# A hybrid encoder layer on one core: the feed-forward in two phases, and an opening without GpSimd

## The chip, the core and the metric

The kernel runs on one core of a Trainium2 chip. The core has a matrix engine (TensorE, PE in the profile, with its weight loads shown apart as PEld), three engines for elementwise work (VectorE = DVE, ScalarE = ACT, GpSimd = POOL) and a queue engine (SyncE = SP) that here issues every transfer between device memory (DRAM) and the on-chip memory (SBUF). Matmul results go to eight banks of an accumulation memory (PSUM), from which DVE and ACT copy them. The metric is device time in microseconds, the median of some runs; lower is better. The profile is one further execution.

## What is computed

One layer of an encoder for 1024 prompt tokens and 8 x 16 sample tokens, all treated as 1152 rows of width 1024 in single precision. An input layer norm, one wide projection, three mixers, a merge and a layer norm come first; then the convolutional feed-forward, which the change is about. From the reference:

```python
def causal_dwconv(u, buf, w):
    width = w.shape[0]
    t = u.shape[1]
    full = jnp.concatenate([buf.astype(u.dtype), u], axis=1)
    out = full[:, 0:t] * w[0]
    for j in range(1, width):
        out = out + full[:, j:j + t] * w[j]
    return out, full[:, t:]
...
    x = layer_norm(ALPHA * x + mix @ w_out, ln1_g, ln1_b)

    up, new_ffn_conv = causal_dwconv(x @ w_up, buf_ffn, f_conv_w)
    gate, val = jnp.split(up + f_conv_b, 2, axis=-1)
    x = layer_norm(ALPHA * x + (jax.nn.silu(gate) * val) @ w_down, ln2_g, ln2_b)
```

`w_up` is 1024 x 5632 (2816 gate and 2816 value columns), `w_down` is 2816 x 1024.

## The kernel before

**Tiles.** Rows (tokens) come in three blocks of 384 (`n`, 0 to 2), features in pieces of 128. Every matrix product is made of three matmuls on numbers split in two: high part times high part, low times high, high times low. A split is a cast on one engine (the high part) and a subtraction (the low part). A projection block (`block`, for one 128-column piece of weights and one row block) is 8 x 3 = 24 matmuls of 128x128 by 128x384. A weight piece is loaded raw (`wraw`, two buffers), cast by ACT (L205) and subtracted by DVE (L206) into `whl` (two buffers).

**Order.** Code is written in program order with side generators (`beside`) that advance one step at each `tick`, that is after every second contraction step of the matmuls. A planner then orders the instructions of each engine by its own simulation of time; within an engine, and within the SP queue, the order is fixed at build time and each instruction waits for its inputs and for the buffers that it overwrites.

**Opening** (L126 to L445). Nine row tiles of x are loaded (`load_x`, tag `xt`, six buffers). For each third, `ln_in` takes statistics on DVE (`ln_group`, L319 to L308), normalises (DVE for the first two tiles of the first third, else ACT), and `to_features` (L336) transposes on PE (L147), scales on ACT (L343), casts on DVE (L344) and subtracts on DVE and POOL in turn (L345). The first two projection units (`q_unit`) run in the order unit 0, unit 1 for each third, two PSUM banks (`g`) between them. The statistics of the second third are tied to follow the small operations of the first (`issue_after(ready[-1])`).

**Feed-forward** (L1658 to the end). For each of 22 pairs (128 gate columns, 128 value columns), the evictions `ev_half` copy the block to `xp` (ACT, L1743), convolve (ACT L1759, DVE L1762 twice), apply SiLU (L1765), multiply (DVE, L1769) and split the product into `g` tiles (L1773, L1774), which stay in SBUF (24 buffers). After two pairs of up-projection, `down` multiplies the two pairs before them with their rows of `w_down` (`late`, two split weight tiles) and adds the result to the residual sum `yac` (L1807). For one row tile and one half of the columns that is 2 x 3 matmuls of 128x128 by 128x512. The last `down` takes four pairs, adds with a row sum (L1817), and `last_ln` follows for each row tile: ACT and DVE for the first eight, and for the last one a chain on DVE and ACT with high priority (L1855 to L1864), with its stores at the end. `residual` loads the rows of the first norm back into `yac` and scales them (L1689, L1690) right after the first four up-projection blocks.

Of the kernel before, what the change touches and what calls it, by code (L numbers as in the profile page):

```python
# [71 lines left out]
def tile_encoder_step(ctx: ExitStack, tc: tile.TileContext, cst, x_prompt, x_sample, cache_k, cache_v, st_hgrn,  # L72
# [8 lines left out]
    wp = ctx.enter_context(tc.tile_pool(name="wp", bufs=2))  # L81
    s0 = ctx.enter_context(tc.tile_pool(name="s0", bufs=16 * NBLK))
# [85 lines left out]


# [3 lines left out]
    def vec_rows(items):  # L173
        with tc.tile_pool(name=nm("vst"), bufs=1) as vst:
            st = vst.tile([96, P], F32, name=nm("vstage"))
            r0 = sum(nv)
            r = 0
            for n, ap in items:
                k = ap.shape[0]
                load(st[r:r + k, :], ap)  # L180
                vo[n] = r0 + r
                r += k
            nv.append(r)
            ps = psum("ms")
            tr(ps[:, :r], st[:r, :])
            V.tensor_copy(vec[:, r0:r0 + r], ps[:, :r])
# [12 lines left out]
    def prep(pieces, kt=KD, cols=P):  # L199
# [4 lines left out]
        hl = wp.tile([P, 2, KD, P], F32R, tag="whl", name=nm("whl"), bufs=2)  # L204
# [27 lines left out]
    def block(hl, xh, xl, n, evict, kt=KD):  # L232
# [3 lines left out]
        for k in range(kt):  # L236
# [98 lines left out]

    def to_features(pool, xns, n, gname, bname, hi, lo):  # L336

        for k in range(KD):
# [6 lines left out]
            (G if k % 2 else V).tensor_sub(lo[k][n], x32, hi[k][n].bitcast(F32))  # L345
# [11 lines left out]
    def ln_in(n):  # L357
# [3 lines left out]
        for i, (t, (mu, rs)) in enumerate(zip(xts, st)):  # L361
            nb, r = (ln_st[:, 3 * n + i, j:j + 1] for j in range(2))
            if n == 0 and i < 2:
                V.tensor_scalar(t, t, mu, rs, ALU.subtract, ALU.mult)
            V.scalar_tensor_tensor(nb, mu, -1.0, rs, ALU.mult, ALU.mult)
            last = V.tensor_copy(r, rs)
            if n or i == 2:
                S.activation(t, t, AF.Identity, bias=nb, scale=r)  # L368
        ready.append(last.ins)
        yield from to_features(lambda: lp.tile([P, NW], F32, tag="x32", name=nm("x32"), bufs=4), xts, n, "ling", "linb",  # L370
                               hh, hl_)

# [1286 lines left out]
    late = ExitStack()  # L1659
# [17 lines left out]
    late_w = lambda: fp.tile([P, 2, D], F32R, tag="late", name=nm("late"), bufs=2)  # L1677
    yac = []

    def residual():  # L1680
        gb = late_w().bitcast(F32)
        for i, src in enumerate((ln1_g[0], ln1_b[0])):
            load(gb[:, i], src.partition_broadcast(P))
        yield 2
        S.mul(gb, gb, ALPHA)
        for j in range(NT):
            yac.append(yp.tile([P, D], F32, name=f"yac{j}"))
            load(yac[j], d_xn1[j * P:(j + 1) * P, :])
            V.tensor_mul(yac[j], yac[j], gb[:, 0])  # L1689
            V.tensor_add(yac[j], yac[j], gb[:, 1])  # L1690
            yield 3


# [18 lines left out]
    def ffn_pair(i):  # L1712
        pr = Head()
        pr.gate, pr.l36 = {}, None
        pr.gh, pr.gl = [None] * NBLK, [None] * NBLK

        def tail():
            yield 5
            ps1 = psum("ms")
            tr(ps1[:36, :P], pr.l36)  # L1720
            r36 = fp.tile([36, P], F32, tag="r36", name=nm("r36"), bufs=1)
            V.tensor_copy(r36, ps1[:36, :P])
            for hf in range(2):
                c0 = hf * DFF + i * P
# [3 lines left out]
        def ev_half(half):  # L1728
            st = {}
            ct = half * NFF + i  # L1730

            def ev(n, ps):
                last = n == NBLK - 1
                w = FW - 2 if last else NW
                xp = fpiece("xp", 3, FW)
                if n == 0:
                    V.memset(xp[:, 0:2], 0.0)
                    if half == 0 and i % 4 == 0:
                        beside(ffn_states(i))
                else:  # L1740
                    V.tensor_copy(xp[:, 0:2], st["carry"])
                if not last:
                    S.copy(xp[:, 2:2 + NW], ps)  # L1743
                    cr = fpiece("carry", 3, 2)
                    V.tensor_copy(cr, xp[:, NW:NW + 2])
                    st["carry"] = cr
                else:
                    if half == 0:
                        pr.l36 = fpiece("l36", 2, 36)
                    xv = bt(xp[:, 2 + FPW:FW], 2 + TB)  # L1750
                    V.tensor_copy(xv[:, :, 0:2], bt(old[i][half], 2))
                    S.copy(xp[:, 2:2 + FPW], ps[:, :FPW])
                    S.copy(xv[:, :, 2:], bt(ps[:, FPW:]))
                    V.tensor_copy(pr.l36[:, 2 * half:2 * half + 2], xp[:, FPW:FPW + 2])
                    V.tensor_copy(bt(pr.l36[:, 4 + 16 * half:20 + 16 * half], 2), xv[:, :, TB:])
                    if half:
                        beside(tail())
                acc = fpiece("ga", 4, FW) if half == 0 else fpiece("va", 2, FW)
                S.activation(acc[:, :w], xp[:, 2:2 + w], AF.Identity, scale=fvec[:, 2, ct:ct + 1],  # L1759
                             bias=fvec[:, 3, ct:ct + 1])  # L1760
                for j in range(2):
                    V.scalar_tensor_tensor(acc[:, :w], xp[:, j:j + w], fvec[:, j, ct:ct + 1], acc[:, :w],  # L1762
                                           ALU.mult, ALU.add)
                if half == 0:
                    S.activation(acc[:, :w], acc[:, :w], AF.Silu)  # L1765
                    pr.gate[n] = acc
                    return
                ga = pr.gate[n]
                V.tensor_mul(ga[:, :w], ga[:, :w], acc[:, :w])  # L1769
                gh, gl = fpiece("g", 24, NW, F32R), fpiece("g", 24, NW, F32R)  # L1770
                pr.gh[n], pr.gl[n] = gh, gl
                if not last:
                    S.copy(gh, ga[:, :w])  # L1773
                    V.tensor_sub(gl, ga[:, :w], gh.bitcast(F32))  # L1774
                else:
                    S.copy(gh[:, :FPW], ga[:, :FPW])
                    V.tensor_sub(gl[:, :FPW], ga[:, :FPW], gh[:, :FPW].bitcast(F32))
                    gv = bt(ga[:, 2 + FPW:FW], 2 + TB)[:, :, :TB]
                    S.copy(bt(gh[:, FPW:]), gv)
# [155 lines left out]
```

## Time and profile before

| | us |
|---|---|
| median of 3 runs (2264.65 to 2267.57) | 2264.73 |
| profiled execution | 2265.47 |
| its span, first to last instruction | 2263.7 |
| TensorE busy in the span | 2204.9 |
| VectorE busy | 1494.3 |
| ScalarE busy | 957.5 |
| GpSimd busy | 27.4 |

The mean granted clock of TensorE is 0.991 of full speed. The profile names an instruction by the line that issued it, its engine, operation and tiles (output<-inputs); all matmuls share L107 and all transposes L147, since a helper issues them. "Idle before <-X" is how long the engine stood before the instruction, and what ended that. The stretches that matter in the text are the opening (0 to about 60 us), the entry into the feed-forward (about 1430 to 1460), the feed-forward (to 2250) and the tail (from 2250).

### The profile page before, as it was taken

Reading aid. Unit: us, or ns where it says so; the run is one execution under the profiler, and the core shown is the slowest. Engines: PE = TensorE matmul, PEld = TensorE weight load, DVE = VectorE, ACT = ScalarE, POOL = GpSimd, SP = SyncE. Lnnn points to the kernel's source line nnn. Section 1 sums busy time; section 2 is a strip of 40 time slices with the busy share of each in tenths; the row PEclk is TensorE's granted clock in tenths of the full one; section 3 lists DMA queues with packets and bytes.
Section 4 is the critical chain, followed back from the end, with each engine's and each line's share of the span. In section 5 each row is a group of like instructions: output and inputs, shape, how many; then the busy total and the mean of one; then the engine's idle time right before and its main releaser. Section 6 shows DMA issues by size and latency. Waiting matters only on the chain.

```text
span 2263.7 us, 34662 instructions
## 1 busy us (share of the span) xinstructions
PE 2204.9 (97%) x12959; PEld 2060.0 (91%) x12959; DVE 1494.3 (66%) x4292; ACT 957.5 (42%) x2195; POOL 27.4 (1%) x28
## 2 busy tenths in 40 slices
PE   6999989999999999999999899999999999999997
PEld 6998889999999999999989888899999999999996
DVE  8267556666675657767878786776566656655667
ACT  4356434334444436365432333453334323433347
POOL 2000000000000000000000001000000000000000
PEclk9999999999999999999999999999999999999998
DMA  4121231222232221312354542321101110111022
GB/s 135 47 77 53 89 94 47 80 75 62 64 84 61 68 68 41 102 36 68 103 175 131 173 151 75 135 67 49 38 29 58 48 41 28 57 48 48 20 66 85
DMA packets 223929, 168.36 MB, mean 74 GB/s; under 512 B 34650, under 2 KB 213504, under 8 KB 223744
## 3 DMA queue, kind: packets, MB, share of 16 engines
q1 hardware_dynamic: 223760, 166.14, 24.5%
q8 instruction: 102, 1.67, 0.3%
q14 instruction: 67, 0.55, 0.1%
HBM read 126.91 MB, written 40.11 MB: 74 GB/s over the span
## 4 chain that ended last, share of the span: by engine, by line
PE 91%; DVE 4%; ACT 3%; issue 1%; DMA 1%; POOLq 0%; SPq 0%; POOL 0%; DVEq 0%; ACTq 0%
PE psg L107 78%; PE psp L107 5%; PE psch L107 4%; PE psp L147 1%; PE psms L107 1%; PE psch L147 1%; PE psms L147 1%; DMA xp<-d_o 0%; ACT L1199 0%; ACT L1195 0%; DVE o L1455 0%; DVE whl L206 0%; DMA vstage<-in_ln_in_b_dram 0%; ACT k L1195 0%; ACT xt L368 0%
## 5 line engine op out<-in xcount | busy, mean ns | idle before, releaser
L107 PE MATMUL psg<-hh,whl 128*128 128x384 f32 x2976 | 809.2, 345 | 1.4 <-DVE r27c L823 0.7
L107 PEld LDWEIGHTS psg<-hh,whl 128*128 128x128 f32 x2976 | 536.2, 189 | 15.3 <-issue 8.6
L107 PE MATMUL psg<-x1h,whl 128*128 128x384 f32 x2112 | 543.7, 336 | 0.9 <-ACT whl L205 0.9
L107 PE MATMUL psg<-hl,whl 128*128 128x384 f32 x1488 | 509.0, 342 | 1.2 <-POOL hl L345 1.2
L107 PEld LDWEIGHTS psg<-x1h,whl 128*128 128x128 f32 x2112 | 383.4, 188 | 3.3 <-ACT whl L205 1.4
L107 PE MATMUL psg<-x1l,whl 128*128 128x384 f32 x1056 | 354.8, 336 | 2.3 <-POOL x1l L345 1.3
L107 PEld LDWEIGHTS psg<-hl,whl 128*128 128x128 f32 x1488 | 280.6, 189 | 6.1 <-issue 2.6
L107 PE MATMUL psg<-late,g 128*128 128x512 f32 x1080 | 251.1, 391 | 0.0
L107 PEld LDWEIGHTS psg<-late,g 128*128 128x128 f32 x1080 | 201.9, 188 | 42.8
L107 PEld LDWEIGHTS psg<-x1l,whl 128*128 128x128 f32 x1056 | 199.3, 189 | 3.3 <-POOL x1l L345 1.6
L206 DVE TENSOR_TENSOR whl<-wraw,whl 128x1024 fp32r<-128x1024 f32 (+1 forms) x122 | 140.6, 1153 | 62.4 <-ACT whl L205 60.8
L1807 DVE TENSOR_TENSOR yac<-yac,psg 128x512 f32<-128x512 f32 x164 | 112.8, 688 | 89.7 <-PE psg L107 86.1
L107 PE MATMUL psg<-o,whl 128*128 128x384 f32 x720 | 141.7, 348 | 5.1 <-ACT o L1454 2.8
L205 ACT CAST whl<-wraw 128x1024 fp32r<-128x1024 f32 (+1 forms) x122 | 121.4, 996 | 59.7 <-PE psg L107 40.1
L107 PEld LDWEIGHTS psg<-o,whl 128*128 128x128 f32 x720 | 126.7, 193 | 7.7 <-ACT o L1454 3.4
L1762 DVE SCALAR_TENSOR_TENSOR va<-xp,fvec,va 128x384 f32<-128x384 f32 x132 | 82.0, 621 | 19.8 <-ACT va L1759 18.1
L107 PE MATMUL psg<-wres,mixh 128*128 128x512 f32 x288 | 92.3, 394 | 0.0
L1762 DVE SCALAR_TENSOR_TENSOR ga<-xp,fvec,ga 128x384 f32<-128x384 f32 x132 | 81.5, 619 | 11.6 <-ACT ga L1759 9.9
L1791 ACT CAST late<-wraw 128x1024 fp32r<-128x1024 f32 x20 | 20.1, 1047 | 162.5 <-PE psg L107 162.5
L1743 ACT COPY xp<-psg 128x384 f32<-128x384 f32 x88 | 42.2, 480 | 108.4 <-PE psg L107 108.0
L1421 ACT ACTIVATE ga<-psg 128x384 f32<-128x384 f32 x72 | 35.4, 491 | 99.3 <-PE psg L107 76.6
L854 DVE SCALAR_TENSOR_TENSOR acc<-xp,vec,acc 128x384 f32<-128x384 f32 (+1 forms) x108 | 64.8, 619 | 3.2 <-ACT acc L852 2.7
(468 smaller groups left out, 3104.3 us busy)
## 6 DMA issues: line engine op xcount, KB each, us to landing
wraw<-in_w_in_dram SPq DMA_DIRECT2D x58, 512.0 KB
wraw<-in_w_up_dram SPq DMA_DIRECT2D x44, 512.0 KB
d_g<-ga SPq DMA_DIRECT2D x72, 192.0 KB
wraw<-in_w_down_dram SPq DMA_DIRECT2D x22, 512.0 KB
acc<-d_g SPq DMA_DIRECT2D x48, 192.0 KB
d_o<-sq SPq DMA_DIRECT2D x24, 192.0 KB
xp<-d_o SPq DMA_DIRECT2D x24, 192.0 KB
x<-d_g SPq DMA_DIRECT2D x24, 192.0 KB
```

The source lines that it names most:

```text
L107: PE.matmul(out, lhsT, rhs, start=start, stop=stop)
L147: PE.transpose(out, in_, ident[:n, :n])
L205: S.copy(hl[:, 0, :kt, :cols], raw[:, :kt, :cols])
L206: V.tensor_sub(hl[:, 1, :kt, :cols], raw[:, :kt, :cols], hl[:, 0, :kt, :cols].bitcast(F32))
L854: V.scalar_tensor_tensor(acc[:, :w], xp[:, j:j + w], vcol("gcw", 12 * j + ci), acc[:, :w], ALU.mult, ALU.add)
L1421: S.activation(g, ps, AF.Tanh, scale=0.5)
L1743: S.copy(xp[:, 2:2 + NW], ps)
L1762: V.scalar_tensor_tensor(acc[:, :w], xp[:, j:j + w], fvec[:, j, ct:ct + 1], acc[:, :w], ALU.mult, ALU.add)
L1791: S.copy(hl[:, 0], raw)
L1807: V.tensor_add(yac[j][:, cs], yac[j][:, cs], ps)
```

## The change

The feed-forward becomes two phases. In the first, all 44 up-projection units run, and each pair's gated product is stored to DRAM (`d_gu`, 22 tensors of 128 x 1152). Then the pools of the first phase (`wp`, `s0`, `fp`) are closed and a pool `dp` and eight PSUM banks (`g`) are opened. The second phase makes two passes over the 22 row pieces of `w_down`, eleven each; a pass takes the three row blocks in turn, loads and splits the gated pieces (`gr`, `gd`), and keeps six sums in PSUM, for three row tiles and two column halves, over all eleven pieces. Weights are loaded and split at the first row block of a pass (`wdr`, `wd`, 12 buffers). The last row block of the second pass goes one sum at a time. `residual` moves to the second phase; the last norm's affine vectors are two whole tiles.

In the opening the low part is always subtracted on DVE; the statistics of the next third are tied to follow the last split of this one; `xt` has four buffers; the first three units run third by third, two of them interleaved by contraction step (`two_blocks`), with a third weight tile; the first tile of each third is normalised on ACT, the others on DVE; 20 matmuls on a constant come first; one copy moves from DVE to ACT, and the memsets of two masks move from DVE to GpSimd.

```diff
+    wp_ctx, s0_ctx = ExitStack(), ExitStack()
...
-            xts.append(lp.tile([P, D], F32, tag="xt", name=nm("xt"), bufs=6))
+            xts.append(lp.tile([P, D], F32, tag="xt", name=nm("xt"), bufs=4))
...
+    for _ in range(2):
+        ps = psum("g")
+        for i in range(10):
+            mm(ps[:, :P], ones, ones)
...
-            V.tensor_copy(vec[:, r0:r0 + r], ps[:, :r])
+            S.copy(vec[:, r0:r0 + r], ps[:, :r])
...
+    def two_blocks(hls, xh, xl, n, evicts):
+
+        os_ = [psum("g")[:, :NW] for _ in range(2)]
+        for k in range(KD):
+            for o, hl, evict in zip(os_, hls, evicts):
+                mm(o, hl[:, 0, k, :], xh[k][n], start=(k == 0), stop=False)
+                mm(o, hl[:, 0, k, :], xl[k][n], start=False, stop=False)
+                mm(o, hl[:, 1, k, :], xh[k][n], start=False, stop=(k == KD - 1))
+                if k == KD - 1:
+                    evict(n, o)
+            tick()
...
-            (G if k % 2 else V).tensor_sub(lo[k][n], x32, hi[k][n].bitcast(F32))
+            split_last[0] = V.tensor_sub(lo[k][n], x32, hi[k][n].bitcast(F32))
             yield 1
...
-            if n == 0 and i < 2:
+            V.scalar_tensor_tensor(nb, mu, -1.0, rs, ALU.mult, ALU.mult)
+            V.tensor_copy(r, rs)
+            if i == 0:
+                S.activation(t, t, AF.Identity, bias=nb, scale=r)
+            else:
                 V.tensor_scalar(t, t, mu, rs, ALU.subtract, ALU.mult)
...
+        ready.append(split_last[0].ins)
...
-    Q.blocks[:6] = [Q.blocks[i] for i in (0, 3, 1, 4, 2, 5)]
-    Q.weights(0)
+    Q.blocks[:9] = [Q.blocks[i] for i in (0, 3, 6, 1, 4, 7, 2, 5, 8)]
+    first = [Q.weights(0), Q.weights(1)]
+    Q.units[2][1] = Q.units[2][0](lp.tile([P, 2, KD, P], F32R, name="whl3"))
     x_in += [load_x(n) for n in (1, 2)]
-    for n in (1, 2):
-        beside(ln_in(n))
-        Q.run(2)
+    for n in range(NBLK):
+        if n < 2:
+            beside(ln_in(n + 1))
+        evicts = [Q.blocks.pop(0)[4] for _ in range(2)]
+        two_blocks(first, hh, hl_, n, evicts)
+        Q.run(1)
         drain()
...
+        for t in (reset, resets):
+            G.memset(t, 1.0)
+            G.memset(t[:, 0:NW:P], 0.0)
+        G.memset(resets[:, 2 * P::TB], 0.0)
...
+    d_gu = [dram.tile([P, T], F32, name=f"d_gu{i}") for i in range(NFF)]
...
+            xp = self.x[half, n] = fpiece("xp", 5, FW)
...
+            ga = self.gate[n]
+            if not last:
+                V.tensor_mul(ga[:, :w], ga[:, :w], acc[:, :w])
+                store(d_gu[self.i][:, tok(n)], ga[:, :w])
+            else:
+                V.tensor_mul(xp[:, :FPW], ga[:, :FPW], acc[:, :FPW])
+                gv, av = (bt(t[:, 2 + FPW:FW], 2 + TB)[:, :, :TB] for t in (ga, acc))
+                V.tensor_mul(bt(xp[:, FPW:NW]), gv, av)
+                store(d_gu[self.i][:, tok(n)], xp[:, :NW])
...
+    Q.run(4)
+    drain()
+    lnrow.close()
+    Q.run()
+
+    drain()
+    xs_ctx.close()
+    late.close()
+    s0_ctx.close()
+    wp_ctx.close()
+    share_banks(g=8)
+    dp = late.enter_context(tc.tile_pool(name="dp", bufs=1, reuse_waits="tile"))
+    yp = xs_ctx.enter_context(tc.tile_pool(name="yp", bufs=1, side="right", reuse_waits="tile"))
...
+    late_w = lambda: dp.tile([P, 2, D], F32R, tag="wd", name=nm("wd"), bufs=12)
...
+    def prep_step(half, n, k):
+        if n == 0:
+            raw = dp.tile([P, D], F32, tag="wdr", name=nm("wdr"), bufs=2)
+            load(raw, w_down[0, k * P:(k + 1) * P, :])
+            hl = wd[k] = late_w()
+            S.copy(hl[:, 0], raw)
+            V.tensor_sub(hl[:, 1], raw, hl[:, 0].bitcast(F32))
+        raw = dp.tile([P, NW], F32, tag="gr", name=nm("gr"), bufs=3)
+        load(raw, d_gu[k][:, tok(n)])
+        g = gd[k, n] = dp.tile([P, 2, NW], F32R, tag="gd", name=nm("gd"), bufs=13)
+        S.copy(g[:, 0], raw)
+        V.tensor_sub(g[:, 1], raw, g[:, 0].bitcast(F32))
+
+    def terms(ps, k, n, i, cs, first, stop):
+        g, sl = gd[k, n], slice(i * P, (i + 1) * P)
+        mm(ps, g[:, 0, sl], wd[k][:, 0, cs], start=first, stop=False)
+        mm(ps, g[:, 1, sl], wd[k][:, 0, cs], start=False, stop=False)
+        mm(ps, g[:, 0, sl], wd[k][:, 1, cs], start=False, stop=stop)
...
+    three_halves = dp.tile([P, 1], F32, name="three_halves")
+    V.memset(three_halves, 1.5)
+    cols = [slice(hf * 512, (hf + 1) * 512) for hf in range(2)]
+    rows_of = [range(0, NFF // 2), range(NFF // 2, NFF)]
+    steps = [(half, n, k) for half in range(2) for n in range(NBLK) for k in rows_of[half]]
...
+    at = 0
+    for half, ks in enumerate(rows_of):
+        for n in range(NBLK):
+            if (half, n) == (0, 0):
+                prepare(3)
+                beside(residual())
+            if (half, n) != (1, NBLK - 1):
+                acc = [(i, hf, psum("g")) for i in range(3) for hf in range(2)]
+                for k in ks:
+                    prepare(min(at + 8, 3 + 2 * at))
+                    at += 1
+                    for i, hf, ps in acc:
+                        terms(ps, k, n, i, cols[hf], k == ks[0], k == ks[-1])
+                        if k == ks[-1]:
+                            put_sum(half, 3 * n + i, hf, ps)
+                        if hf:
+                            tick()
+            else:
+                prepare(len(steps))
+                for i in range(3):
+                    for hf in range(2):
+                        ps = psum("g")
+                        for k in ks:
+                            terms(ps, k, n, i, cols[hf], k == ks[0], k == ks[-1])
+                            if k % 2:
+                                tick()
+                        put_sum(half, 3 * n + i, hf, ps)
```

`prepare(upto)` calls `prep_step` for the steps up to that number; `put_sum` adds a finished sum to `yac` and, in the second pass, takes the row sum and starts `last_ln`.

More of the change, by code (lines that the diff above doesn't have):

```diff
@@ L1676, in tile_encoder_step @@
     FW = 2 + FPW + NB * (2 + TB)
[L1677 to L1691, printed above, removed]
+    d_gu = [dram.tile([P, T], F32, name=f"d_gu{i}") for i in range(NFF)]
     old = {}
@@ L1723, in tail @@
             for hf in range(2):
-                c0 = hf * DFF + i * P
+                c0 = hf * DFF + self.i * P
                 store(p_fconv[0, 0, :, c0:c0 + P], r36[2 * hf:2 * hf + 2, :])
                 store(s_fconv[0, :, :, c0:c0 + P].rearrange("b j c -> (b j) c"), r36[4 + 16 * hf:20 + 16 * hf, :])
-        def ev_half(half):
-            st = {}
-            ct = half * NFF + i
-            def ev(n, ps):
[L1733 to L1779, printed above, removed]
-                    V.tensor_sub(bt(gl[:, FPW:]), gv, bt(gh[:, FPW:]).bitcast(F32))
-            return ev
@@ L1784, in ffn_pair @@
-        for half in range(2):
-            Q.unit(lambda half=half: prep_cols(w_up[0], 0, KD, half * DFF + i * P), xh, xl, ev_half(half))
-        return pr
-    def prep_down(ff, hl):
-        raw = wp.tile([P, D], F32, tag="wraw", name=nm("wraw"), bufs=2)
-        load(raw, w_down[0, ff * P:(ff + 1) * P, :])
-        S.copy(hl[:, 0], raw)
-        V.tensor_sub(hl[:, 1], raw, hl[:, 0].bitcast(F32))
-        return hl
-    def down(prs, hls, then=None, total=None):
-        for j in range(NT):
-            n, sl = j // 3, slice(j % 3 * P, (j % 3 + 1) * P)
-            for hf in range(2):
-                cs = slice(hf * 512, (hf + 1) * 512)
-                row_block([p_.gh[n][:, sl] for p_ in prs], [p_.gl[n][:, sl] for p_ in prs],
-                          lambda i, k: hls[k][:, i, cs],
-                          lambda ps: (total or add)(j, hf, cs, ps))
-            if then is not None:
-                then(j)
@@ new lines, in ev, with units @@
+        def ev(self, half):
+            def ev(n, ps):
+                if n == 0 and half == 0 and self.i % 4 == 0:
+                    beside(ffn_states(self.i))
+                self.put(half, n, ps)
+                self.conv(half, n)
+            return ev
+        def units(self):
+            for half in range(2):
+                Q.unit(lambda half=half: prep_cols(w_up[0], 0, KD, half * DFF + self.i * P), xh, xl, self.ev(half))
+    pairs = [Pair(i) for i in range(NFF)]
+    for pr in pairs:
+        pr.units()
@@ new lines, in tile_encoder_step @@
+    Q.blocks[:6] = [Q.blocks[i] for i in (0, 1, 3, 4, 2, 5)]
+    Q.run(4)
[10 more added lines that the diff above has]
+    yp = xs_ctx.enter_context(tc.tile_pool(name="yp", bufs=1, side="right", reuse_waits="tile"))
+    yac = [yp.tile([P, D], F32, name=f"yac{j}") for j in range(NT)]
+    wd, gd = {}, {}
@@ L1889, in tile_encoder_step @@
-    yp = late.enter_context(tc.tile_pool(name="yp", bufs=1, side="right", reuse_waits="tile"))
-    beside(residual())
-    for i in range(0, NFF, 2):
-        if i:
-            hls = [prep_down(i - 2 + k, late_w()) for k in range(2)]
-        Q.run(4 * NBLK if i else 4 * NBLK - 4)
-        if 0 < i < NFF - 2:
-            down(pairs[i - 2:i], hls)
-    hls += [prep_down(NFF - 2 + k, wp.tile([P, 2, D], F32R, tag="whl", name=nm("whl"), bufs=2)) for k in range(2)]
-    load_ln2()
-    three_halves = fp.tile([P, 1], F32, name="three_halves")
@@ new lines, in tile_encoder_step, with prepare, put_sum @@
+    ahead = [0]
+    def prepare(upto):
+        while ahead[0] < min(upto, len(steps)):
+            prep_step(*steps[ahead[0]])
+            ahead[0] += 1
+    def put_sum(half, j, hf, ps):
+        if half == 0 or j == NT - 1:
+            V.tensor_add(yac[j][:, cols[hf]], yac[j][:, cols[hf]], ps)
+        else:
+            add_and_sum(j, hf, cols[hf], ps)
+        if half and hf:
+            beside(last_ln(j))
+    at = 0
[15 more added lines that the diff above has]
+                            tick()
+            else:
+                prepare(len(steps))
[7 more added lines that the diff above has]
+                        put_sum(half, 3 * n + i, hf, ps)
```

148 lines of the change are left out of this document (87 added, 61 removed).

## The prediction

> **What bounds the kernel now.** I read the page's busy shares first, then the busy time by stretch, then the timeline and the waits of the stretches where TensorE is not full.
>
> ```profile
> span 2263.7 us, 34662 instructions
> PE 2204.9 (97%) x12959; PEld 2060.0 (91%) x12959; DVE 1494.3 (66%) x4292; ACT 957.5 (42%) x2195; POOL 27.4 (1%) x28
> ...
> 0.00:60.00 60.00, 41.87 (x235) 36.58 (x236) 46.97 (x142) 30.87 (x45) 13.94 (x16) 1.00 0.45 128
> ...
> 1500.00:2200.00 700.00, 700.00 (x3744) 659.80 (x3743) 427.87 (x915) 246.81 (x458) 0.00 (x0) 1.00 0.15 44
> ...
> 2249.90:2263.70 13.80, 0.00 (x0) 0.00 (x0) 9.91 (x26) 7.63 (x21) 0.00 (x0) 0.58 0.37 142
> ```
>
> The columns of the last three rows are stretch, length, busy time of PE, PEld, DVE, ACT and POOL, granted clock, DMA share, GB/s. TensorE is the bound, and from 1500 to 2200 us, which is nearly all of the feed-forward, it has no idle time: 700 of 700. Busy says nothing of pace, so I check that:
>
> ```profile
> 1600.05 0.33 PE L107 MATMUL psg<-x1l,whl 128*128 128x384 f32 x1
> ...
> 1600.57 0.33 PE L107 MATMUL psg<-x1l,whl 128*128 128x384 f32 x1
> ...
> 2210.97 1.54 PE L107 MATMUL psg<-late,g 128*128 128x512 f32 x6
> ...
> 2213.74 1.54 PE L107 MATMUL psg<-late,g 128*128 128x512 f32 x6
> ```
>
> Three up-projection matmuls (two x1h lie between these rows) take 1600.57 - 1600.05 = 0.52 us, 0.173 each; twelve of the down-projection (six more between) take 2213.74 - 2210.97 = 2.77, 0.231 each: 0.45 ns a column in both. The change keeps all 3168 + 1188 of them, in the same two shapes, with one weight load each. So the two-phase order has nothing to win inside the feed-forward. It can win only where PE stands or runs slowly: the opening (60 - 41.87 = 18.1 us idle), the entry into the feed-forward, the tail (13.8). And it adds a new place to lose: the handover between the phases.
>
> **The change part by part.** Negative is a gain.
>
> *Opening.*
>
> ```profile
> L107 PE MATMUL psg<-hh,whl 128*128 128x384 f32 x97 | 26.4, 344 | 0.0
> L107 PE MATMUL psg<-hl,whl 128*128 128x384 f32 x48 | 16.8, 350 | 1.2 <-POOL hl L345 1.2
> L345 POOL TENSOR_TENSOR hl<-x,hh 128x384 fp32r<-128x384 f32 x12 | 13.7, 1144 | 40.9 <-DVE hh L344 27.3 <-DVE nwy L308 8.2 <-DVE nwa L305 1.7
> L343 ACT ACTIVATE x<-psp,vec 128x384 f32<-128x384 f32 x12 | 8.1, 674 | 1.7 <-DVE hl L345 1.1 <-PE psp L147 0.6
> L344 DVE CAST hh<-x 128x384 fp32r<-128x384 f32 x24 | 8.1, 348 | 4.7 <-ACT x L343 4.6
> L364 DVE TENSOR_SCALAR xt<-xt,lnmv,nwy 128x1024 f32<-128x1024 f32 x2 | 1.6, 809 | 0.0
> ...
> 11.41 0.16 DVE L306 SCALAR_TENSOR_TENSOR nwa<-nwa,lnvr 128x3 f32<-128x3 f32 x1
> ...
> 14.78 3.65 DVE L319 BATCH_NORM_STATS2 lnst<-xt 128x6 f32<-128x512 f32 x6
> ...
> 39.49 0.97 DVE L306 SCALAR_TENSOR_TENSOR nwa<-nwa,lnvr 128x3 f32<-128x3 f32 x1
> 40.38 0.55 DVE L345 TENSOR_TENSOR hl<-x,hh 128x384 fp32r<-128x384 f32 x1
> ```
>
> The same tiny L306 takes 0.16 us alone and 0.97 beside a POOL split: POOL's twelve splits of 1.14 us hold up DVE, so giving them to DVE at 0.55 costs it little. Now the pace. By 60 us PE has 97 + 48 projection matmuls plus 16 narrow ones behind it (161 x 0.173 = 27.9 us) and 72 transposes (0.107 at full pace, 7.7): 35.6 us of work, 24.4 lost. After the change a third of the tokens costs DVE 3.65 (statistics) + about 3.3 (an estimate: some 18 small ones like L306, 0.16 to 0.2 each) + 1.6 (two normalisations, L364) = 8.6 us, then 8 features of 0.35 + 0.55, overlapped to about 0.87: 7.0 us; the statistics of the next third stand behind the last split of this one. The first third is normalised near 13 us as now; the next third's statistics no longer run ahead of its features (14.78, 3.65 long), so its matmuls start some 3 us earlier, near 16. DVE's order then gives features done at 23.5, 40 and 56.7; PE has 3 blocks of 24 matmuls (12.4 us) per third, waits between the thirds, and ends the third third at 56.7 + 1.0 + 4.15 = 61.9, with 216 x 0.173 + 7.7 = 45.1 us of work done. The kernel before gets there at 60 + 9.5 = 69.5. That is -7.6. Against it: the input has four buffers instead of six, so the last rows load only after transposes (+1), both PSUM banks of the projection empty together (+0.5), and a clock drop in one of two gaps (+0.6 in the mean): **-5.5**, between -8 and +1.5. The memsets moved to POOL and the vector copy moved to ACT are 0.4 us or less and lie beside DMA waits: 0.
>
> The 20 warm-up matmuls run while PE waits anyway, until 12.67. What they could buy is the pace of the first transposes:
>
> ```profile
> 13.15 0.42 PE L147 MATMUL psp<-call,xt 128*128 128x128 f32 x1
> 13.37 0.42 PE L147 MATMUL psch<-call,xt 128*128 128x128 f32 x1
> ...
> 30.70 0.27 PE L147 MATMUL psp<-call,xt 128*128 128x128 f32 x1
> 30.82 0.27 PE L147 MATMUL psch<-call,xt 128*128 128x128 f32 x1
> ```
>
> They are 0.21 us apart at first, 0.11 later: half pace. ACT's 0.67 us per feature (L343) is longer than three of them at either pace, so I take 0 (bounds -1 to +0.3).
>
> *Entry into the feed-forward.*
>
> ```profile
> PE psg L107 <- POOL x1l L345: 1.3, 1, 1.3
> PE psg L107 <- DVE x1l L345: 1.0, 1, 1.0
> PE psg L107 <- ACT whl L205: 0.9, 1, 0.9
> ...
> 1444.33 2.24 POOL L345 TENSOR_TENSOR x1l<-x,x1h 128x384 fp32r<-128x384 f32 x1 [3.00 <-DVE x1h L344]
> ...
> 1446.60:1453.20 6.60, 5.65 (x16) 5.14 (x17) 4.74 (x9) 4.10 (x8) 0.00 (x0) 0.50 0.85 322
> ```
>
> PE stands 3.2 us here, and then runs 6.6 us at a granted clock of 0.50, which costs (6.6 - 0.9)/2 = 2.8 more: 6.0 in all. The split that POOL did in 2.24 takes DVE 0.55, so the 1.3 goes, the clock drop probably with it, and the residual's 18 DVE passes leave this place too. What is late next is the DVE split before it and the weight cast, 1.9 together. **-3.5**, between -6 and +2 (DVE is the queue for all of it).
>
> *Handover.* Second-phase tiles lie where first-phase tiles lay, each waiting for those below it. Counting declared sizes in order of first use, the first weight tile lies on both weight buffers of the first phase (32 bytes on the second one), so its cast waits for the very last up-projection matmul; the first raw and split gated tiles lie on convolution buffers, which are free only when the last pair is through. The same steps of today's last pair:
>
> ```profile
> 2195.77 0.48 ACT L1743 COPY xp<-psg 128x384 f32<-128x384 f32 x1 [0.20 <-PE psg L107]
> ...
> 2198.34 0.56 DVE L1769 TENSOR_TENSOR ga<-ga,va 128x384 f32<-128x384 f32 x1
> ...
> 2198.93 0.51 ACT L1773 CAST g<-ga 128x384 fp32r<-128x384 f32 x1 [1.93 <-DVE ga L1769]
> ...
> 2187.88 1.06 ACT L1791 CAST whl<-wraw 128x1024 fp32r<-128x1024 f32 x1
> ...
> 2188.97 1.23 DVE L1792 TENSOR_TENSOR whl<-wraw,whl 128x1024 fp32r<-128x1024 f32 x1 [0.77 <-PE psg L107]
> ...
> 0.74 1.34 SPq L110 DMA_DIRECT2D xt<-in_x_prompt_dram  x3
> ...
> 4.29 1.29 DVE L319 BATCH_NORM_STATS2 lnst<-xt 128x6 f32<-128x512 f32 x2 [3.29 <-DMA xt<-in_x_prompt_dram]
> ```
>
> Lower end: 1.06 + 1.23 = 2.3 us of weight split, no clock drop. Upper end: 3.1 from block end to product (2195.77 to 2198.90), a store and a load at 3.5 each (0.74 to 4.29, a larger one), 0.5 of cast, so 10.6, and 2.8 of clock: 13.4. Between: the raw tile is loaded, the split waits for the product, 3.1 + 0.5 + 0.6 + 0.5 in line = 4.7, and with the clock drop seen at the entry 2.8: **+7.5**, the case nearest to the rows of the last pair. The Trainium skill, "TensorE: Matmul & The Clock Gate", Part 1, has the full clock back after about 3.4 us of sustained matmuls; by that rule a drop costs 1.7 (an estimate from that page), not 2.8, and the sum below would be -6.0. The entry's row, 6.6 us at half clock, speaks against it.
>
> *Second phase.* Each of the 22 steps that brings weights needs 512 + 192 KB in 18 x 0.231 = 4.2 us, 172 GB/s, plus ACT 1.06 + 0.51 and DVE 1.23 + 0.56: all below the step. 36 sums of 0.69 replace 180; PE did not wait for them between 1500 and 2200 us. 66 stores of 192 KB lie beside up-projection matmuls. 0, if the loads land in time (rival 1).
>
> *Tail.*
>
> ```profile
> 2249.91 0.69 DVE yac L1807
> ...
> 2252.44 1.54 DVE L1862 SCALAR_TENSOR_TENSOR yac<-yac,lnmv,ln2v 128x384 f32<-128x384 f32 x3
> ...
> 2254.23 1.02 DVE L1880 TENSOR_TENSOR yac<-yac,ln2v 128x384 f32<-128x384 f32 x2
> ...
> 2255.80 0.21 ACT nwa L1830
> ...
> 2258.74 1.54 DVE L1864 SCALAR_TENSOR_TENSOR yac<-yac,nwy,ln2v 128x384 f32<-128x384 f32 x3 [0.43 <-ACT nwy L1833]
> ```
>
> From 2249.91 to 2260.3 the last row block's norm takes 10.4 us because the affine passes of the rows before it (L1880 and the like) sit in between. With 66 matmuls a row block (15 us) instead of 24 these are through. What stays is 0.69 + 0.69 + 0.21 + 0.35 of small ones, ACT's chain 2258.74 - 2255.80 = 2.9, and 1.54: 6.4, or 7.9 if the three L1862 go first. Gain 2.5 to 3.9: **-3.4**.
>
> *Sum.* -5.5 - 3.5 + 7.5 - 3.4 = -4.9. The profiled execution took 2265.47 us (its span is 2263.7; 1.8 lie around it), so 2260.6 against it, and 2259.8 against the median 2264.73.
>
> **The rivals.**
>
> 1. *Slower: second-phase loads starve PE.* Two raw weight buffers: each is loaded (3.5 us), cast (1.06) and subtracted (1.23), 5.8 us, or 2.9 per step against 4.2. It decides once a load lands later than 8.4 - 2.3 = 6.1 us after issue. At 8 us a step takes 5.2, and 22 steps lose 21 us: about 2281. For: all loads and stores share SP's queue, in order, behind waiting ones. Against: today's loads reach 322 GB/s in the stretch 1446.60:1453.20 above. 0.14.
>
> 2. *No difference.* PE's gaps between the thirds of the opening, some 3 to 4 us each, drop the clock as the entry did; half pace makes a feature's six matmuls 2.1 us, longer than DVE's 0.85, and both thirds lose 2.8: the opening falls to about 0, and the sum is +0.6: 2265. 0.28.
>
> 3. *More gain: a short handover.* If the slots that the first gated tile gets belong to an earlier pair, only the weight split is left, 2.3 to 2.7 us, with no clock drop: 2.5 instead of 7.5, so 2254.8. Which slot the planner hands out decides; three of the four gate buffers belong to the last pair, which speaks against. The drop at the entry came after scattered waits of 1.0 and 1.3, so a short gap may not be safe either. The Trainium skill, "TensorE: Matmul & The Clock Gate", Part 1, would have a gap under its idle window keep the clock; that the entry's drop came after less is what the trace has against it. 0.20.
>
> That the planner undoes the change (hoists nothing, or keeps the old opening order) is inside the forecast's spread.
>
> **How the numbers follow.** Forecast 0.38, rivals 0.14, 0.28, 0.20. About 0.2% (4.5 us) is what a measurement of this kernel can tell from no change. The forecast lies just past it: 0.25 of its 0.38 count as faster, 0.13 as same. Rival 3 is faster; rival 2 is same but for 0.03 slower. Faster 0.45, same 0.38, slower 0.17. The range takes the lower ends of opening and handover (-8 + 2.3 - 3.5 - 3.4, 2252, less 2 for the entry) up to handover and opening both at their upper halves (+11 - 2 - 1.5 - 3, 2269): 2250 to 2270, leaving out rival 1.
>
> **What would show it.** Right: no POOL splits; PE starting on projections near 16 us and ending the third third near 62 to 65; near 1445 no wait on POOL and the clock above 0.9; one gap of about 5 us near 1985 with a clock of 0.5 behind it; 0.231 us per matmul after it; about 10 us after the last matmul instead of 13.8. Wrong: several gaps after the handover (rival 1), or half pace in the opening (rival 2).

## The result and the profile after

| | before | after |
|---|---|---|
| median, us | 2266.15 (2264.65 to 2268.03, 4 runs) | 2280.26 (2278.94 to 2281.3, 4 runs) |
| ratio, 95% interval | | 1.0067 (1.0055 to 1.008) |
| profiled span, us | 2263.7 | 2279.0 |

The change makes the kernel 14.1 us slower; 2259.8 was forecast, and the range ended at 2270. The head of the page of after, then the busy time by stretch (stretch, length, busy time of PE, PEld, DVE, ACT, POOL, granted clock, DMA share, GB/s):

```profile
span 2279.0 us, 34962 instructions
...
PE 2211.8 (97%) x12999; PEld 2066.3 (91%) x12999; DVE 1391.4 (61%) x4082; ACT 950.4 (42%) x2171; POOL 1.3 (0%) x9
```

```profile
0.00:60.00 60.00, 48.98 (x288) 45.73 (x289) 47.67 (x143) 26.19 (x40) 1.30 (x9) 0.97 0.49 131
...
30.00:36.00 6.00, 3.80 (x26) 3.12 (x26) 3.64 (x16) 3.40 (x6) 0.00 (x0) 1.00 0.00 0
...
1446.60:1453.20 6.60, 6.60 (x40) 6.53 (x39) 5.57 (x13) 2.95 (x6) 0.00 (x0) 1.00 1.01 406
...
1981.97:1985.40 3.43, 3.43 (x8) 2.75 (x9) 2.79 (x4) 1.89 (x3) 0.00 (x0) 0.50 0.99 295
1985.40:1989.00 3.60, 3.60 (x17) 2.92 (x17) 0.71 (x2) 0.83 (x2) 0.00 (x0) 0.99 1.03 411
2001.79:2005.20 3.41, 3.41 (x8) 2.76 (x9) 3.41 (x4) 0.00 (x0) 0.00 (x0) 0.50 0.82 258
2005.20:2009.00 3.80, 3.80 (x16) 3.07 (x16) 3.80 (x6) 1.47 (x2) 0.00 (x0) 0.90 0.76 270
...
2267.90:2279.00 11.10, 0.00 (x0) 0.00 (x0) 4.97 (x13) 2.65 (x9) 0.00 (x0) 0.69 0.14 47
```

The places the change was to help are better. Of the 288 PE records in the first 60 us 40 are the warm-up matmuls (6.96 us), which leaves 248 against 235 before: some 2 us ahead. The entry (1446.60 to 1453.20) is full and at full clock, and the tail is 11.1 us long instead of 13.8. The loss is new, and lies behind 1972. The waits of PE from 1960 to the end (engine and tile that waited, the releaser, us in total, times, the longest):

```profile
PE psg L108 <- DVE wd L1846: 10.5, 2, 7.0
PE psg L108 <- ACT gd L1850: 7.9, 1, 7.9
PE psms L148 <- DVE l L1754: 0.8, 1, 0.8
```

And the timeline of after there, rows of PE, SP, ACT and DVE put in order of time (start, us, engine, line, operation, tiles, and in brackets the idle time before it and what ended that):

```profile
1972.57 0.34 PE L108 MATMUL psg<-x1h,whl 128*128 128x384 f32 x1
...
1976.31 0.34 SPq L111 DMA_DIRECT2D d_gu<-xp  x1
1976.70 0.43 SPq L111 DMA_DIRECT2D wdr<-in_w_down_dram  x1
...
1979.56 0.44 SPq L111 DMA_DIRECT2D gb<-in_ln_b_dram  x1
...
1980.46 1.04 ACT L1845 CAST wd<-wdr 128x1024 fp32r<-128x1024 f32 x1 [6.22 <-DMA wdr<-in_w_down_dram]
...
1981.97 12.80 PE L108 MATMUL psg<-wd,gd 128*128 128x512 f32 x48 [7.93 <-ACT gd L1850]
...
1988.35 1.92 ACT L1827 ACTIVATE gb<-gb 128x2048 f32<-128x2048 f32 x1 [2.77 <-DMA gb<-in_ln_b_dram]
1990.17 1.03 ACT L1845 CAST wd<-wdr 128x1024 fp32r<-128x1024 f32 x1
...
1990.30 10.31 DVE L1831 TENSOR_TENSOR yac<-yac,gb 128x1024 f32<-128x1024 f32 x9 [4.13 <-ACT gb L1827]
2000.52 1.22 DVE L1846 TENSOR_TENSOR wd<-wdr,wd 128x1024 fp32r<-128x1024 f32 x1
...
2001.79 10.41 PE L108 MATMUL psg<-wd,gd 128*128 128x512 f32 x36 [7.02 <-DVE wd L1846]
...
2006.46 1.06 ACT L1845 CAST wd<-wdr 128x1024 fp32r<-128x1024 f32 x1 [13.07 <-DMA wdr<-in_w_down_dram]
2006.47 8.03 DVE L1832 TENSOR_TENSOR yac<-yac,gb 128x1024 f32<-128x1024 f32 x7
2014.42 1.22 DVE L1846 TENSOR_TENSOR wd<-wdr,wd 128x1024 fp32r<-128x1024 f32 x1
...
2015.69 252.16 PE L108 MATMUL psg<-wd,gd 128*128 128x512 f32 x1104 [3.49 <-DVE wd L1846]
```

Three gaps, not one. In the first (1972.9 to 1981.97, 9.1 us) the loads of the second phase are issued only behind the last pair's store at 1976.31; SP first issues the weight load (1976.70), ACT casts it when it has landed (1980.46). In the other two (7.02 and 3.49) the weight tile has been cast well before (at 1991.20 and 2007.52, by the two casts that begin at 1990.17 and 2006.46). What releases PE is the subtraction L1846 on DVE, and that stands in DVE's order behind nine multiplications (10.31 us) and then seven additions (8.03 us) of the residual, L1831 and L1832. Ahead of the multiplications DVE itself stands 4.13 us, since the first norm's vectors (`gb`) have to land and be scaled first; so the block of passes both begins late and is long. Behind the first two gaps the clock is 0.50 for 3.4 us, and behind the third it is low too (0.57 from 2015.69 to 2019.10). The row of the groups of after from 1972 to 2268 sums it up (busy us, mean ns | idle before):

```profile
L108 PE MATMUL psg<-wd,gd 128*128 128x512 f32 x1188 | 275.4, 395 | 18.4 <-DVE wd L1846 10.5 <-ACT gd L1850 7.9
```

The same 1188 matmuls take 269.57 us where the clock stays full (the ninth experiment below), so half clock took 275.4 - 269.6 = 5.8 us, some 2 for each gap. With the 0.84 us wait and the 0.29 us transpose at the end of the first phase that is 18.4 + 1.1 + 5.8 = 25.3 us lost between the phases, against gains elsewhere of about 10.

### The profile page after: what moved, and what is told of

Read it like the earlier page. It is cut to its first block, busy times and chain, and to the rows that moved or that the text cites. A ratio compares the mean times of both kernels' runs of the same rounds, so it can differ in the third digit from the quotient of the medians.

```text
span 2279.0 us, 34962 instructions
## 1 busy us (share of the span) xinstructions
PE 2211.8 (97%) x12999; PEld 2066.3 (91%) x12999; DVE 1391.4 (61%) x4082; ACT 950.4 (42%) x2171; POOL 1.3 (0%) x9
## 4 chain that ended last, share of the span: by engine, by line
PE 90%; DVE 4%; ACT 3%; DMA 2%; issue 1%; SPq 0%; DVEq 0%; ACTq 0%
PE psg L108 77%; PE psp L108 5%; PE psch L108 4%; PE psp L148 2%; PE psms L108 1%; PE psch L148 1%; PE psms L148 1%; DMA xp<-d_o 0%; DVE yac L1832 0%; ACT L1223 0%; DMA gb<-in_ln_b_dram 0%; ACT L1219 0%; DMA x<-d_g 0%; DVE yac L1831 0%; DVE mix L1518 0%
## 5 line engine op out<-in xcount | busy, mean ns | idle before, releaser
L108 PE MATMUL psg<-wd,gd 128*128 128x512 f32 x1188 | 275.4, 395 | 18.4 <-DVE wd L1846 10.5
L108 PEld LDWEIGHTS psg<-wd,gd 128*128 128x128 f32 x1188 | 226.5, 191 | 67.0 <-DVE wd L1846 11.4
L1851 DVE TENSOR_TENSOR gd<-gr,gd 128x384 fp32r<-128x384 f32 x66 | 36.1, 554 | 85.8 <-ACT gd L1850 85.8
L1850 ACT CAST gd<-gr 128x384 fp32r<-128x384 f32 x66 | 33.3, 512 | 100.5 <-PE psg L108 93.6
L1766 DVE COPY xp<-xp 128x2 f32<-128x2 f32 x88 | 14.9, 169 | 88.5 <-ACT xp L1742 87.5
```

Source lines behind the costliest of these rows:

```text
L108: PE.matmul(out, lhsT, rhs, start=start, stop=stop)
L1766: V.tensor_copy(xp[:, 0:2], self.x[half, n - 1][:, NW:NW + 2])
L1850: S.copy(g[:, 0], raw)
L1851: V.tensor_sub(g[:, 1], raw, g[:, 0].bitcast(F32))
```

## The experiments

All ratios are against runs of the kernel before on the same chip. Its medians there were 2265.4 to 2265.9 us.

| | median, us | ratio (95%) | gaps of PE behind 1972, us |
|---|---|---|---|
| e1_vector_early | 2265.97 | 1.0001 (0.9992 to 1.001) | 8.1 |
| e2_steps_ahead | 2265.13 | 0.9995 (0.9985 to 1.0005) | 0.4, 3.0, 0.5 |
| e3_both | 2259.77 | 0.997 (0.9959 to 0.9981) | 0.4, 0.7 |
| e4_opening_only | 2260.99 | 0.9974 (0.9965 to 0.9982) | (no second phase) |
| e5_dve_split | 2262.92 | 0.9988 (0.9979 to 0.9997) | (no second phase) |
| e6_no_passes | 2266.31 | 1.0001 (0.9992 to 1.0009) | 7.9 |
| e7_phases_only | 2284.45 | 1.0081 (1.0067 to 1.0094) | 8.0, 5.3, 2.6, 0.3, 3.0 |
| e8_tail_order | 2259.09 | 0.9975 (0.9964 to 0.9985) | 0.4, 0.9 |
| e9_kept_warm | 2265.3 | 1.0001 (0.9992 to 1.001) | 0.4 |

Every kernel with a second phase also has the wait of 0.8 us ahead of the last transpose, which the table leaves out.

The theory (Q) was that the residual's 18 passes block DVE's in-order queue ahead of the weight splits. Its rival (T) was that the second phase's loads come too late or too slowly, as rival 1 of the prediction had it.

**The residual's vectors loaded early.** The tile of the first norm's vectors comes from the pool on the right side, which is free when the first phase begins, so that its loads and the passes can be moved forward.

```diff
-        gb = dp.tile([P, 2, D], F32, name="gb2")
+        gb = yp.tile([P, 2, D], F32, name="gb2")
```

> The changed kernel with one edit: the residual's vector tile (gb) comes from the pool on the right side of SBUF, which is free since the entry, so that its two loads and the 18 DVE passes can run beside the up-projection. Theory Q (queue: the 18 passes of 1.14 us, held up by a vector that lands at 1988, stand in DVE's order ahead of the weight splits that TensorE waits for): the gaps of 7.0 and 3.5 us after the handover go, with about 4 us of half clock that follow them; 2280.3 - 14.4 = about 2266, between 2263 and 2268. Theory T (transfers: the second phase's loads land too late for two raw buffers, whatever DVE does): the gaps stay, waits on DMA take their place; 2276 or more.

Its timeline (DVE, then PE):

```profile
1449.27 1.22 DVE L1831 TENSOR_TENSOR yac<-yac,gb 128x1024 f32<-128x1024 f32 x1 [0.68 <-ACT gb L1827]
...
1477.13 1.21 DVE L1832 TENSOR_TENSOR yac<-yac,gb 128x1024 f32<-128x1024 f32 x1
...
1980.95 272.21 PE L108 MATMUL psg<-wd,gd 128*128 128x512 f32 x1188 [8.06 <-ACT gd L1850]
```

All 18 passes now run between 1449 and 1478, beside up-projection matmuls. PE has no wait at all in the 1188 matmuls behind the first gap. One line is worth 14.3 us (2280.26 to 2265.97): two gaps of 10.5 us in all and their two clock drops. That fits Q. It does not exclude T by itself, since the loads of the vectors and of the residual's rows have left the handover too; the experiment without the passes below does.

**The first steps prepared ahead.** A small pool opened in the first phase holds the raw tiles and the first three steps' split tiles; three steps are prepared before the last six up-projection blocks.

```diff
+    pre = pre_ctx.enter_context(tc.tile_pool(name="pre", bufs=1, side="right", reuse_waits="tile"))
...
+    Q.run(len(Q.blocks) - 6)
+    prepare(3)
     Q.run()
```

> The changed kernel with the tiles of the first three steps of the second phase, and the raw buffers, in a pool of their own that is open before the last six up-projection blocks, and those three steps prepared there. Theory P (pool: nothing of the second phase can be loaded until the last convolution ends and its pool closes, so that 9.0 us pass between the last up-projection matmul and the first down-projection one): the first gap falls to 1 us or less and its half clock goes, 9 to 10 us; the residual's passes still block DVE, so some of it may come back in the second gap: 2270 to 2276. Theory T: the first gap shrinks by the first load alone (4 us), the others grow; 2276 or more.

Its timeline:

```profile
1974.99 32.13 PE L108 MATMUL psg<-wd,gd 128*128 128x512 f32 x140 [0.37 <-DVE r L1731]
...
1984.69 10.31 DVE L1858 TENSOR_TENSOR yac<-yac,gb 128x1024 f32<-128x1024 f32 x9 [4.18 <-ACT gb L1854]
...
2010.08 19.27 PE L108 MATMUL psg<-wd,gd 128*128 128x512 f32 x76 [2.95 <-DVE wd L1819]
```

The first gap is gone, and it gave more than was expected of it, 15.1 us: the block of residual passes is still there in one piece (1984.69, 10.31 us), but when it begins five steps of 18 matmuls are split, 90 in all, and PE has made 43 of them: some 47 are in hand, about 11 us. In the changed kernel 4.5 us were in hand (1990.30 to 1994.77). The same passes in the same place, behind the same wait for the vectors (4.18 us), cost 3 us instead of 10.5. So the cost of the passes depended on how little was in store.

**Both.**

> Both edits. Q and P together: no gap over 1 us after the handover, full clock; 2280.3 - 14.4 - 9.7 = about 2256, between 2253 and 2260, faster than the kernel before. Theory T: 2270 or more.

Measured 2259.77, inside the expectation. PE goes from the last transpose of the first phase to the last matmul with waits of 0.38 and 0.69 us, and the clock stays at 1.00. Though the edit is the sum of the two above, the residual's rows were not loaded earlier here (probably because the new pool takes the place on the right side; no run tests that). The passes run from 1984 to 2012, mixed with the splits, and do little harm: the wait of 0.69 us is for a weight split among them.

**The opening alone.** The opening of after (order of blocks, splits on DVE alone, four buffers, warm-up matmuls) with the feed-forward of before.

> The kernel before with the opening of the change alone (everything up to the feed-forward, POOL's splits included); its feed-forward, with the residual at the entry, is the old one. Theory S (the entry gains because POOL no longer takes splits): -0.9 by the start of the up-projection and most of the 4.8 us at the entry; 2261 to 2263. Theory R (the entry gains because the residual's passes left it): only about -1, 2264 to 2266.

Measured 2260.99, at the edge of what theory S gave, and clearly less than theory R's 2264. PE's waits at the entry are 2.3 us instead of 3.2, and the clock there is 1.00.

**The splits alone.** The kernel before with one edit.

```diff
-            (G if k % 2 else V).tensor_sub(lo[k][n], x32, hi[k][n].bitcast(F32))
+            V.tensor_sub(lo[k][n], x32, hi[k][n].bitcast(F32))
```

> The kernel before with one edit: VectorE does all the low-part splits, GpSimd none; the old order of the opening, the residual at the entry and the interleaved feed-forward stay. Theory S (most of what the opening part of the change gives comes at the entry into the feed-forward, where a GpSimd split of 2.24 us held up TensorE): about 2262 us (2260 to 2264), the entry's waits 3.2 down to about 2.4 and the clock there above 0.9, though the opening's order is the old one. Rival (the gain of 4.9 us measured for the whole opening part is the reordered opening itself): within 1 us of the kernel before, 2265 to 2267.

**The two phases alone.** The opening of before with the feed-forward of after.

> The opening of before (GpSimd splits, six input buffers, the old order) with the changed feed-forward. If the two parts of the change add up (opening -4.9, measured alone): 2280.3 + 4.9, about 2285 us (2283 to 2287), with the same gaps of 9, 7 and 3.5 us at the handover. Rival R (the entry's wait and clock drop came from the residual's passes and loads, which the two phases move away anyway): the opening's part is then worth only its early 1 us, about 2281 us (2280 to 2282.5), and no wait on GpSimd near 1445.

The three tell what each half of the change is worth. The waits and the clock of e5 at the entry:

```profile
PE psg L107 <- ACT whl L205: 1.4, 1, 1.4
PE psg L107 <- DVE x1l L345: 1.0, 2, 0.5
```

```profile
1446.60:1453.20 6.60, 5.01 (x26) 4.41 (x27) 5.36 (x12) 4.51 (x9) 0.00 (x0) 1.00 0.98 359
```

With the residual's loads and passes where they were, taking the splits off GpSimd brings the waits from 3.2 to 2.4 us and the clock from 0.50 to 1.00: 0.8 + 2.8 = 3.6 us by these rows, 2.5 by the medians (0.7 to 4.8 by the interval). The whole opening part is worth 4.9 by the medians (4.1 to 7.9), so the reordered opening adds some 2 us to that. The two phases alone cost 19.1 (15.2 to 21.3); less the opening's 4.9 that is 14.2, and both together measured 14.1: as numbers the parts add up. The traces say that this is in part luck. Rival R asked for 2281 and no wait on GpSimd at the entry. Its time failed (2284.45), but its mechanism holds there. The waits and the clock of e7 at the entry, with the splits still on GpSimd and the residual gone:

```profile
PE psg L108 <- ACT whl L206: 1.2, 1, 1.2
PE psg L108 <- POOL x1l L346: 0.3, 1, 0.3
```

```profile
1446.60:1453.20 6.60, 6.54 (x37) 6.21 (x38) 5.87 (x12) 4.28 (x9) 0.00 (x0) 1.00 1.01 390
```

So either edit alone, the splits off GpSimd or the residual moved away, brings the entry to full clock, and with the residual away the splits are worth only 0.3 us of waits there. By the two profiles e7 is 4.3 us longer than the changed kernel for other reasons: 1.0 us until the last matmul ahead of the feed-forward, 0.7 in the first phase, and 2.5 in the second, where its gaps and clock drops came out worse. Why they did, no run shows. Its main gaps behind 1972, in the view of waits of PE:

```profile
PE psg L108 <- ACT gd L1827: 8.0, 1, 8.0
PE psg L108 <- DVE wd L1823: 7.8, 2, 5.3
PE psg L108 <- DVE yac L1916: 3.0, 1, 3.0
```

**The passes left out.** The changed kernel without the lines L1831 and L1832.

> The changed kernel without the 18 VectorE passes that scale the residual by the first norm's vectors (left out: that scaling; its vectors are still loaded and scaled on ScalarE, the residual's rows still loaded). Theory Q (the residual's passes hold up VectorE's in-order queue ahead of the weight splits): the two later gaps of 7.0 and 3.5 us go, the first of about 9 stays: about 2266 us (2263 to 2268), as with the vectors loaded early. Rival T (the second phase's loads, those of the vectors among them, arrive too late): the later gaps stay as waits on weight tiles behind loads, 2276 us or more.

Measured 2266.31. PE's timeline has one stretch behind the first gap:

```profile
1978.67 272.26 PE L108 MATMUL psg<-wd,gd 128*128 128x512 f32 x1188 [7.91 <-ACT gd L1848]
```

The loads of the vectors and of the residual's rows are where they were, at the handover, and none of the later gaps is left: Q holds, T falls. But the edit takes two things away from DVE at once, the 20.6 us of passes and the 4.13 us in which it stood for the vectors ahead of them; no run tells how the gaps divide between the two.

**The tail's order.** In e3's kernel the three wide passes of the last row tile are tied to follow the small ones of the Newton steps.

```diff
-                for sl in thirds:
-                    V.scalar_tensor_tensor(y[:, sl], y[:, sl], mu, g2[:, sl], ALU.subtract, ALU.mult)
+                with tc.issue_after(small[0].ins):
+                    [V.scalar_tensor_tensor(y[:, sl], y[:, sl], mu, g2[:, sl], ALU.subtract, ALU.mult) for sl in thirds]
```

> The kernel with both repairs (steps prepared ahead, vectors early) and the last row tile's three wide VectorE passes made to follow the small ones of its Newton steps, so that ScalarE's chain of 2.98 us runs beside them. Theory (the tail's shortfall is those 1.53 us of passes ahead of ScalarE's chain): the stretch from the last matmul to the last instruction 11.2 down to about 9.7 us, and about 2258.3 us (2256 to 2261) in all. Rival (the stores after the last pass set the tail, or the passes only move behind the chain): no change in that stretch, 2259.8.

Its timeline of DVE:

```profile
2249.95 0.15 DVE L1886 TENSOR_SCALAR nwi<-nwi 128x1 int32<-128x1 int32 x1
2250.02 1.53 DVE L1917 SCALAR_TENSOR_TENSOR yac<-yac,lnmv,gb 128x384 f32<-128x384 f32 x3
2253.08 1.54 DVE L1919 SCALAR_TENSOR_TENSOR yac<-yac,nwy,gb 128x384 f32<-128x384 f32 x3 [1.53 <-ACT nwy L1895]
```

The wait for ScalarE's chain ahead of the last passes is 1.53 us instead of 2.98, and from the last sum (2247.88) to the end of the span (2257.7) it is 9.8 us instead of 11.2. In the median that can't be told from e3.

**The clock term by itself.** The kernel of e1 with 40 matmuls on the constant tile in the gap that is left.

```diff
+    warm = psum("g")
+    for i in range(40):
+        mm(warm[:, :P], ones, ones)
```

> The changed kernel with the vectors loaded early and 40 matmuls of 128x128 on the constant in the handover's gap of 8.06 us (they compute nothing that is used; 40 instructions of them took 6.96 us at half clock at the opening, which by this is about 7 us for 80 at full clock). Theory (the gap costs its length plus half of about 3.4 us, because the granted clock is 0.50 only for the first 3.4 us behind it): the clock stays at 1.00 behind the gap, the 1188 matmuls take about 270.6 us instead of 272.2, and the time is about 2264.4 us (2262 to 2266). Rival (the slow start has another cause, such as weights arriving late, or the prediction's 2.8 us of clock): the 1188 matmuls take 272.2 as before, or 269.4.

Its timeline, and the clock by stretch of e1 for comparison:

```profile
1975.85 9.20 PE L108 MATMUL psg<-ones 128*128 128x128 f32 x80 [0.38 <-DVE r L1731]
1984.81 269.57 PE L108 MATMUL psg<-wd,gd 128*128 128x512 f32 x1188
```

```profile
1980.95:1984.35 3.40, 3.40 (x8) 2.75 (x9) 2.60 (x4) 1.87 (x3) 0.00 (x0) 0.50 0.61 202
1984.35:1987.75 3.40, 3.40 (x11) 2.69 (x11) 2.10 (x4) 1.49 (x3) 0.00 (x0) 0.68 0.84 308
```

Kept busy through the gap, PE does the 1188 matmuls in 269.57 us instead of 272.21. So the half clock behind e1's gap cost 2.64 us: the theory of 1.6 was too small, the prediction's 2.8 about right. The extra matmuls took 9.0 us (0.112 for each of the 80 records, not the 0.087 that was expected); with a wait of 0.38 ahead of them the 1188 begin 1.3 us later behind the first phase than in e1, so that in the median e9 can't be told from e1.

## Why the prediction was wrong

By its own steps:

| step | forecast, us | measured, us |
|---|---|---|
| opening | -5.5 | -0.8 by these two profiles, some -1.7 by all |
| entry into the feed-forward | -3.5 | -4.8 (waits 3.2 to 1.2, clock 2.8) |
| handover | +7.5 | +9.1 idle, +2 clock |
| second phase | 0 | +10.5 idle, +4 clock, -2 pace |
| tail | -3.4 | -2.7 |

**The step that failed** is "Second phase ... 0, if the loads land in time". It counted for each step DVE's weight and gated splits, 1.23 + 0.56 us, and found them below the step's 4.2 us. It left out what the change moves to that place. The prediction says of the entry that "the residual's 18 DVE passes leave this place too", and never says where they arrive: 18 passes of some 1.15 us are 20.6 us of DVE, five steps' worth, ahead of splits that PE needs at once, and DVE stands 4.13 us for their vectors before the first of them. Rows for it stood in the trace of before (in the view of the tile `yac`: count, shortest, median and longest in ns, first and last start):

```profile
L1689 DVE TENSOR_TENSOR yac<-yac,late x9: 1204/1210/1221, 1450.3 to 1470.0; 128x1024 f32<-128x1024 f32 x9
L1690 DVE TENSOR_TENSOR yac<-yac,late x9: 1207/1211/1222, 1454.4 to 1478.2; 128x1024 f32<-128x1024 f32 x9
```

The experiments e1 and e6 show it from two sides: moved away or left out, 10.5 us of waits and their clock drops go. The range left out rival 1's number, 2281. The time came out there, but by another mechanism: with the passes gone (e6) the same raw buffers kept up.

**The handover** was mis-sized: 11 instead of 7.5, inside its bounds of 2.3 to 13.4. The sum of 4.7 us took the first raw tile as loaded while the last product was made. In fact the pool for it opens only when the last convolution has let go of the one before, and SP issues the load behind the last store, so the product (to 1976.24), the load (1976.70 to 1980.46) and two casts (to 1981.92) come one behind another; the subtraction is not waited for. e2 removes that by a pool opened earlier, with the three steps prepared ahead; which of the two counts it does not tell. Rival 3, a short handover, was not the case.

**The opening** was right in its mechanism and too large. Projections begin at 16.54 (near 16 was forecast), and the gaps at the border of two thirds are short:

```profile
13.15 0.69 PE L148 MATMUL psp<-call,xt 128*128 128x128 f32 x2 [4.44 <-ACT xt L387]
...
32.92 0.44 PE L148 MATMUL psp<-call,xt 128*128 128x128 f32 x2 [1.71 <-ACT xt L387]
...
51.35 0.44 PE L148 MATMUL psp<-call,xt 128*128 128x128 f32 x2 [1.71 <-ACT xt L387]
...
63.58 0.44 PE L108 MATMUL psg<-hh,whl 128*128 128x384 f32 x1 [0.22 <-ACT qf L436]
```

The thirds come 51.35 - 32.92 = 18.4 us apart, where the forecast had 16.6 (features done at 23.5, 40 and 56.7). So the last block of the third third begins at 63.58 and ends 4.15 later at 67.7, not at 61.9, against the 69.5 taken for before. The term was the spacing of the thirds. DVE's statistics of two thirds begin 17.3 us apart (24.53 and 41.84), of which DVE stands 2.15 for the first scaled feature, a wait that the forecast's 8.6 + 7.0 us left out; and ACT normalises its tile 1.1 us later behind the statistics in the third third. Rival 2 fails: the clock in the gap from 30 to 36 is 1.00. The warm-up matmuls gave nothing, as forecast: PE stood 4.4 us behind them. The last matmul ahead of the feed-forward comes at 1414.8 to 1416.5 in the profiles with the old opening (three) and at 1410.7 to 1415.6 in those with the new (eight), 1.7 apart in the mean; in the two profiles compared here, 0.8. The eight have the same code up to there and scatter by 4.9 us, so a gain of this size is not settled by single profiles.

**The entry** was right: no wait on GpSimd, full clock. The prediction named both edits that help there, and e5 and e7 show that either alone is enough for the full clock: without GpSimd splits the waits are 2.4 us, without the residual 1.5, with both edits 1.2. **The tail** was 0.7 short, and e8 shows why: the wide passes go ahead of the small ones that ScalarE's chain needs, which was the 7.9 case of the prediction rather than 6.4. **The pace** was forecast at 0.231 us a matmul; at full clock the second phase has 269.57/1188 = 0.227. Over the whole feed-forward that shows as 2 us: before took 835.1 from 1414.8 to 2249.9, 6.0 of it the entry's loss, so 829.1; after took 558.9 - 1.2 for the first phase and 269.6 for these, 827.3.

What the two phases are worth when mended: e3 and e8 take 0.997 and 0.9975 of the time before, the opening alone 0.9974. So the mended two-phase order adds nothing that can be measured to the opening. No run has the mended phases with the old opening, so it stays open how much they would gain without it.

## What to carry to other kernels

When a change moves a step, write down for each engine what the step issues and which instructions stand behind it in the new place; 20 us of an engine at 60% use are free in the middle of a stage and not at its start, where nothing is in store. At a border between phases, look for the first allocation of the second phase: its loads can't begin before that memory is let go of, so give the first steps a place of their own and have several steps ready. A wait that seems to need faster loads may be a ready tile behind other work; see in the timeline what the releasing engine did just before.

## What the runs showed of the hardware

The clock drop behind a gap is not one price. Behind gaps of 7.9 and 7.0 us the granted clock was 0.50 for 3.4 us and then 0.99 and 0.90; in e1, behind 8.06, it was 0.50 for 3.4 us and still 0.68 in the next 3.4, and cost 2.64 us in all; even the gap of 3.04 in e7 brought it to 0.65, while the one of 2.58 there left it at 1.00:

```profile
2047.98:2051.40 3.42, 3.42 (x10) 2.79 (x11) 3.40 (x6) 0.12 (x1) 0.00 (x0) 0.65 0.20 58
```

The Trainium skill, "TensorE: Matmul & The Clock Gate", Part 1, has a free-running window of about 3.4 us, after a busy one of which the clock is full again, so that the point of change varies with the phase. A stretch of half clock between one window and two, 1.7 to 3.4 us lost (an estimate from that page), fits 2.64 and the 2 of after's gaps. In the prediction the entry's 6.6 us at half clock was held against that rule; it has a second gap inside it (0.9 us, `whl` in the waits), so it said less than was made of it. That the clock fell at that entry behind waits of 1.0 and 1.3 us, while e5 and e4 kept it with waits of 0.5, 0.4 and 1.4, no run here explains.

GpSimd's splits held up even small operations of VectorE. In the opening of before, L306 took 0.147 to 1.002 us; in e5, without them, all nine take 0.154 to 0.163, as the group of e5 shows for their mean:

```profile
L306 DVE SCALAR_TENSOR_TENSOR nwa<-nwa,lnvr 128x3 f32<-128x3 f32 x9 | 1.4, 159 | 0.2
```

The Trainium skill, "SBUF — State Buffer", "SBUF: two separate sides", calls the port pair that the two engines share an exclusive lock, held for the whole instruction; the L306 of 1.002 us, which began at 27.05 beside a split that took 1.01 us from 27.03, agrees.
